# Idle TensorE products ahead of two expert stages, and the modulation sums of the first mixer at other chunks

## The chip, the cores and the metric

The kernel runs on one core of a Trainium2 chip. The metric is the device time of one launch in microseconds. Below, TensorE does the products (PE in the profile, PEld its weight loads), VectorE is DVE, ScalarE is ACT, GpSimd is POOL, and SyncE (SP) issues most of the transfers. Line numbers such as L862 are those of the kernel before.

## The reference, cut to what matters

A backbone of two layers over 512 latent tokens and 256 context tokens, each a row of 1024 numbers. Layer 0 mixes with a Fourier step beside a gated convolution, layer 1 with windowed attention. Each layer ends in a mixture of 32 experts, of which a token uses two. Each layer's shifts, scales and gates come from a modulation vector.

```python
for layer in range(2):
    mod_l = silu(c) @ w_mod[layer] + b_mod[layer]          # six vectors of 1024
    mod_c = silu(c_ctx) @ w_mod[layer] + b_mod[layer]
    hl = modulate(rms_norm(xl, norm_mix_g[layer]), sh1_l, sc1_l)
    # layer 0: p = h @ w_in; y = concat(fourier(a), b * conv(c * hv)) @ w_out
    # layer 1: windowed attention of latent queries, with the context keys in the same softmax
    xl = xl + g1_l * yl
    hl2 = modulate(rms_norm(xl, norm_ffn_g[layer]), sh2_l, sc2_l)
    f = hier_moe(hl2, ...)   # best group of 4, best two of its 8 experts, by two small products
    # each expert: (silu(x @ w1[e]) * (x @ w3[e])) @ w2[e], times the token's gate
    xl = xl + g2_l * f
```

Layer 0 does the same to the context rows. The inputs and outputs are fp32.

## The kernel before, in words

**First mixer.** `proj` multiplies the split weights (a high part `whi` by ScalarE, the rest `wlo` by VectorE, L1253 and L1255) with the split rows. First come four Fourier chunks (`for g in range(4)`, L1309), each with a projection `four_a` and, one chunk later, the transforms `four_b`; then four convolution chunks (`for j in range(4)`, L1330) with three projections each. Between them sit two feeds that work out modulation vectors. `ModFeed.step` (L1037) multiplies a 2 MB block of `w_mod` on TensorE; it has 16 steps. `SumFeed` does the latent half of four vectors of layer 1 on VectorE: each of its 32 steps adds one 512 KB slice of `w_mod`, times a number, into `acc` (L1075), and after eight steps `finish` sums over the partitions with four small products (L1088), adds the bias (L1090) and writes the vector to memory. Both feeds get their blocks through GpSimd's queue, in the order of issue, and a block is requested when the buffer of an earlier one has been read.

**Mixer output and router.** `mixer_out` multiplies with the output weights, tile by tile of 128 tokens, and does for each tile the norm, the router's products (L223) and, in `Route.tiles`, the choice of experts. `Route.tiles` has three parts with a `yield` between them: VectorE makes the masks `M` and their sum `Mb` (to L341); TensorE counts ranks (L347) and VectorE makes one-hot rows from them (L349 to L357); TensorE sums the first slots' tokens into `acc` (`slots`, L281). `tokens` turns that into a table, and `rest`, later, does the other slots, the gates and the expert numbers (L407, L408). `in_order` chains TensorE's and VectorE's instructions there in program order; for what stands outside it, a scheduler with a cost model picks the order.

**Expert stage.** `moe` goes through the experts in pairs (layer 1 has three groups of four as well). Rows are fetched for 128 slots: in layer 0 by an indirect transfer on GpSimd (`gather`, L739), in layer 1 by products with a one-hot matrix (`tokens_slots` L753, `take` L767). `turn` transposes them (L774), then come w1 and w3 (L862), w2 (L933) and the products that add the result to the tokens (L811). Expert weights stream through a ring of eight buffers of 2 MB, two transfers each, all on SyncE's queue (L723) in order; a transfer waits until its buffer has been read, and the first fourteen are also paced, each by the landing of the one two before. For all but the first experts SyncE first loads the expert's number from a table (L706) that `rest` makes. `run` starts a stage.

Of the kernel before, what the change touches and what calls it, by code (L numbers as in the profile page):

```python
# [85 lines left out]
def body(tc, I, out, upto=None, dbg=None):  # L86
# [140 lines left out]
    def carve(*ts):  # L227
# [15 lines left out]

        return f

    class Route:


# [52 lines left out]
        def tiles(self, m0, m1):  # L301

            n, ms = m1 - m0, slice(m0, m1)
            kg, gk, km, d, k, s2 = [x[:, 0:n] for x in (self.kg, self.gk, self.km, self.d, self.k, self.s2)]
            gm, og, mx0, mx1, Mb, Mc = self.gm[:, ms], self.og[:, ms], self.mx[:, 0, ms], self.mx[:, 1, ms], self.Mb, self.Mc
            M, rk = [x[:, :, ms] for x in (self.M, self.rk)]
            R = self.R.rearrange("p c m e -> p (c m e)")[:, 0:n * 64].rearrange("p (c m e) -> p c m e", c=2, m=n)
            lgg = self.lg[:, ms, 0:4]
            le = self.lg[:, ms, 4:36].rearrange("p m (g e) -> p m g e", g=4)

            def w4(a):
                return a[:, :, None].to_broadcast([128, n, 4])

            def w8(a):
                return a[:, :, :, None].to_broadcast([128, n, 4, 8])

            def first():

                V.scalar_tensor_tensor(k.rearrange("p m g e -> p (m g) e"), d.rearrange("p m g e -> p (m g) e"), 0.0,
                                       K("ew")[:, None, :].to_broadcast([128, n * 4, 8]), op0=ALU.is_equal, op1=ALU.mult)  # L320

            V.tensor_reduce(gm, lgg, axis=AX.X, op=ALU.max)
            V.tensor_reduce(mx0, le, axis=AX.X, op=ALU.max)
            V.tensor_tensor(kg, lgg, w4(gm), op=ALU.is_equal)
            V.tensor_sub(d, le, w8(mx0))
            V.tensor_mul(kg, kg, K("gw")[:, None, :].to_broadcast([128, n, 4]))
            first()
            V.tensor_reduce(gk, kg, axis=AX.X, op=ALU.max)
            V.tensor_reduce(km, k, axis=AX.X, op=ALU.max)
            V.tensor_tensor(og, kg, w4(gk), op=ALU.is_equal)  # L330
            for c in range(2):
                V.tensor_tensor(k, k, w8(km), op=ALU.is_equal)
                if c == 0:
                    V.scalar_tensor_tensor(s2, k, -1e30, le, op0=ALU.mult, op1=ALU.add)
                V.tensor_mul(M[:, c].rearrange("p m (g e) -> p m g e", g=4), k, w8(og))
                if c == 0:
                    V.tensor_reduce(mx1, s2, axis=AX.X, op=ALU.max)
                    V.tensor_sub(d, s2, w8(mx1))
                    first()
                    V.tensor_reduce(km, k, axis=AX.X, op=ALU.max)  # L340
            V.tensor_add(Mb[:, ms], M[:, 0], M[:, 1])  # L341
            yield
            pr = self.psum([128, n, 32])
            for m in range(m0, m1):
                w = [(tri, Mb[:, m])] + [(ones, Mb[:, i]) for i in range(m0, m)] + ([(ones, Mc)] if m0 else [])
                for i, (a, b) in enumerate(w):
                    T.matmul(pr[:, m - m0], a, b, start=i == 0, stop=i == len(w) - 1)  # L347
            for c in range(2):
                V.tensor_mul(self.Mv[:, c, 0, ms], M[:, c], K("blk")[:, ms, None].to_broadcast([128, n, 32]))  # L349
            V.tensor_scalar(self.Mv[:, :, 1, ms], M, K("pcol"), None, op0=ALU.mult)  # L350
            V.tensor_mul(R, M, pr[:, None].to_broadcast([128, 2, n, 32]))
            V.tensor_reduce(rk, R, axis=AX.X, op=ALU.add)
            for c in range(2):
                V.tensor_tensor(self.oh[:, c, ms], K("iota")[:, None, 0:64].to_broadcast([128, n, 64]),
                                rk[:, c, :, None].to_broadcast([128, n, 64]), op=ALU.is_equal)
            for m in range(max(m0, 1), m1):
                V.tensor_add(Mc, Mb[:, 0] if m == 1 else Mc, Mb[:, m])  # L357
            yield
            for m in range(m0, m1):
                self.slots(self.acc, m, self.Mv[:, :, :, m], self.early)  # L360
            yield

        def tokens(self):
# [299 lines left out]
    def moe(layer, NT, tb, ring, mp, mps, near):  # L663
# [288 lines left out]
        def run(rest):  # L952
            X[0] = mp.tile([128, 8, 128], F32, name="xt", bufs=2 if both else 1)
            if not near["h2"]:
                near["held"].update({i: gather(0) for i in (13,)})
            one_hot(0)
            if near["h2"]:
                for f in near["lower"]:
                    lo = f()
                    tc.add_manual_dep(lo.ins, near["mark"].ins.name,  # L960
                                      mybir.DependencyInfo(mybir.DependencyClass.NoSync, mybir.DependencyReason.DATA), reason="order")
                    near["mark"] = lo
            oh = tokens_slots(0) if near["h2"] else None
            for hf in range(2):
                xr = take(oh, hf)
            for hf in range(2):
                turn(0, xr, hf)
            if not near["h2"]:
                gather(order[1])
            with tc.issue_after(near["mark"].ins):  # L970
                rest()
            fill()
            for n in range(len(steps)):
                py_ = step(n)
            with in_order(mybir.EngineType.PE, mybir.EngineType.DVE):
                if near["late"]:
                    hi = rows(last, 1, py_, lambda: [add(last, 0, m) for m in range(2)])
                    near["late"](hi, lambda m, hf: add(last, hf, m))
                else:
                    rows(last, 1, py_, lambda: [near["done"](m, 0, add(last, 0, m)) for m in range(2, NT)])  # L980
                    for m in range(NT):
                        near["done"](m, 1, add(last, 1, m))
            if not near["late"]:
                beyond()
# [62 lines left out]
    class SumFeed:  # L1047
# [1 line left out]


        def __init__(self, layer, vectors, room):
            self.layer, self.vectors, self.room = layer, vectors, room
            self.acc = room.tile([128, D], F32, name="acc")
            self.todo = [(v, k) for v in vectors for k in range(8)]
            self.w = []
            self.ld = 0
            for _ in range(2):
                self.load()

        def tile(self):  # L1060
            return self.room.tile([128, D], F32, name="mw", bufs=2)

        def load(self):
            if self.ld < len(self.todo):
# [5 lines left out]
        def step(self):  # L1070
            v, k = self.todo.pop(0)
            self.ld -= 1
            w = self.w.pop(0)
            if k:
                V.scalar_tensor_tensor(self.acc, w, sil[:, k, 0:1], self.acc, op0=ALU.mult, op1=ALU.add)  # L1075
            else:
                V.tensor_scalar(self.acc, w, sil[:, k, 0:1], None, op0=ALU.mult)
            if k == 7:
                self.finish(v)
            self.load()  # L1080

        def finish(self, v):

# [221 lines left out]
    prev = None  # L1305
    load_conv(0)
    pre = proj_pre()
    sums = SumFeed(1, (2, 3, 4, 5), sp)
    for g in range(4):  # L1309
        aT = four_a(g)  # L1310
        if g:
            with tc.issue_after(mm["last"].ins):
                feed.step()
        sums.step()
        if prev is not None:
            four_b(g - 1, prev)
        feed.step()
        sums.step()
        sums.step()
        prev = aT  # L1320
    wo = I["w_out_even"][0].rearrange("(j p) d -> p j d", p=128)

# [7 lines left out]
    for j in range(4):  # L1330
        wr4 = wconv[j]
        pc = proj(lambda k0: wr4[:, k0:k0 + 4, 1, :])
        if prev is not None:
            four_b(3, prev)
            prev = None
            close(fp)
            cp = pool("cp")
            u = cp.tile([128, L + LC + 4], F32, name="ut")
            for c in (0, L + 1, L + 2, L + LC + 3):
                V.memset(u[:, c:c + 1], 0.0)  # L1340
        csb = tp.tile([128, L + LC + 4], F32, name="t3", bufs=2)
        S.copy(csb[:, 0:L + LC], pc)
        feed.step()
        sums.step()
        load_conv(j + 1)
        if j == 3:
            wout = load_wout(0, 1)
# [5 lines left out]
        V.scalar_tensor_tensor(z[:, 1:1 + N2], u[:, 0:N2], cw[:, 0, j:j + 1], z[:, 1:1 + N2], op0=ALU.mult, op1=ALU.add)  # L1353
        V.scalar_tensor_tensor(z[:, 1:1 + N2], u[:, 2:2 + N2], cw[:, 2, j:j + 1], z[:, 1:1 + N2], op0=ALU.mult, op1=ALU.add)
        feed.step()
        sums.step()
        sums.step()
        pb = proj(lambda k0: wr4[:, k0:k0 + 4, 0, :])
        for o, p0, n in segs:
            V.tensor_mul(z[:, o:o + n], z[:, o:o + n], pb[:, p0:p0 + n])  # L1360
        put_y(4 + j, [z[:, o:o + 256] for o in (1, 257, L + 3)])
        feed.step()
        sums.step()
        sums.step()
    close(cp, tp, sp, hp)


    def mixer_out(layer, NT, lhs, raws, whl, x1, psA, psB, hq, rq, mk_route, h2dst, mdp):
# [30 lines left out]
        for hf in range(2):  # L1399
# [67 lines left out]
            with in_order(PE, DVE, chain=chain):  # L1467
# [4 lines left out]
                for g in going:  # L1472
                    for _ in g:
                        pass
        route.md = mds[0]
        route.tokens()
        return route

# [124 lines left out]
    def modulated(m, xn, hf_, psum):  # L1603
# [3 lines left out]
        for hf in range(2):  # L1607
# [7 lines left out]
                else:  # L1615
                    V.tensor_scalar(hf_[:, k, :], p[:, q, :], A1[:, s, k:k + 1], AB[:, s, 0, k:k + 1], op0=ALU.mult, op1=ALU.add)

    near = {"quads": 0, "late": row_scale, "more": kv_weights, "h2": None, "spill": 1, "x1": x1, "xg": mx_[:, 0, :], "grow": [mx_[:, 1, :], mx_[:, 2, :]],
            "iota": slots_iota(mp)}
    G.memset(near["xg"], 0.0)  # L1620
    near["held"] = {13: route.wrote}
# [352 lines left out]
        hs = slice(hf * 512, hf * 512 + 512)  # L1974
        Y.dma_start(out[0, m * 128:(m + 1) * 128, hs], x1[m][:, hs])

    near = {"quads": QUADS, "done": store, "late": None, "held": {}, "h2": h2s, "md": route.md, "lower": route.lower, "spill": 0, "x1": x1, "grow": [mp.tile([128, D], F32, name="grow")], "iota": slots_iota(mp)}
    S.dma_start(near["grow"][0], brow(mod_d[1, 0, 5 * D:6 * D]))
    fill, run = moe(1, 4, tb, ring, mp, mps, near)
    fill(6)  # L1980
# [33 lines left out]
```

## Time and profile before

| what | value |
|---|---|
| median of 3 runs | 1658.29 us (1654.82 to 1658.82) |
| profiled execution | 1657.86 us, of which the span 1655.9 us |
| TensorE busy | 1525.1 us, 92% of the span |
| VectorE busy | 759.7 us, 46% |
| ScalarE busy | 440.3 us, 27% |
| transfers | 503.50 MB, mean 304 GB/s |
| mean granted TensorE clock | 0.965 of 2.4 GHz |

The span runs from the first to the last instruction of the execution that was profiled. Busy shares are averages over stages with different limits: the first mixer runs to about 235 us, its output and router to 350, layer 0's experts to 850, attention to 1100, the second output and router to 1165, layer 1's experts to the end.

### The profile page before, as it was taken

To read this page: it belongs to the slowest core of one execution; us is meant where nothing else is said; L and a number is where in the kernel's file an instruction comes from. 1 tells how busy PE (TensorE), PEld (TensorE's weight loads), DVE (VectorE), ACT (ScalarE), POOL (GpSimd) and SP (SyncE) were. 2 spreads that over 40 slices of the span, in tenths; PEclk is the share of its full clock that TensorE was granted. 3 is DMA by queue.
4 is the path that set the end of the run, shared out by engine and by line. 5 is a ranking of instruction groups with operands and counts; after the bars stand their busy time and mean duration, and the time that the engine had idled before them with its cause. 6 is when DMAs were issued, how large, how long until landed. Compare 5 with 4: busy or idle time off the path is not lost.

```text
span 1655.9 us, 21500 instructions
## 1 busy us (share of the span) xinstructions
PE 1525.1 (92%) x8011; PEld 866.5 (52%) x8011; DVE 759.7 (46%) x1671; ACT 440.3 (27%) x879; POOL 141.7 (9%) x160
## 2 busy tenths in 40 slices
PE   4989997969999999999988989999799999997787
PEld 2757876843444434444447776668444544531332
DVE  4546553784342534333366975555622322320223
ACT  5322221311111111111046577644221222210110
POOL 2522100300000000000033210000000000000000
PEclk9999997979999999999979999999899999998999
DMA  9897672579999999999930121042699999999996
GB/s 387 306 389 246 229 245 82 189 278 424 425 424 424 381 394 424 425 424 424 407 121 1 51 52 52 1 128 76 237 426 427 426 426 427 426 416 427 426 427 260
DMA packets 108832, 503.50 MB, mean 304 GB/s; under 512 B 18784, under 2 KB 33632, under 8 KB 56752
## 3 DMA queue, kind: packets, MB, share of 16 engines
q1 hardware_dynamic: 93600, 447.31, 67.1%
q0 software_dynamic: 11952, 51.55, 8.2%
q10 hardware_dynamic: 3168, 3.17, 0.6%
q8 instruction: 66, 1.08, 0.3%
q14 instruction: 46, 0.38, 0.1%
HBM read 499.30 MB, written 5.32 MB: 305 GB/s over the span
## 4 chain that ended last, share of the span: by engine, by line
PE 34%; DMA 10%; DVE 3%; ACT 2%; issue 1%; SPq 0%; DVEq 0%; ACTq 0%
PE p L862 8%; PE yp L933 5%; DMA w<-in_w_dram 5%; DMA hhi<-in_w_dram 4%; PE A L1715 3%; PE cp L811 3%; PE A L1436 3%; PE tp L767 2%; PE A L1833 2%; PE O L1895 2%; PE B L1880 2%; ACT P L1839 1%; PE tp L774 1%; DVE x L812 1%; DMA w<-in_w_qkv_dram 0%
## 5 line engine op out<-in xcount | busy, mean ns | idle before, releaser
L862 PE MATMUL p<-w,xt 128*64 128x512 f32 (+1 forms) x1024 | 338.5, 611 | 14.3 <-DMA w<-in_w_dram 14.1
L862 PE MATMUL p<-r,xt 128*64 128x512 f32 (+1 forms) x784 | 284.2, 620 | 8.3 <-DMA r<-in_w_dram 7.9
L812 DVE TENSOR_TENSOR x<-x,cp 128x512 f32<-128x512 f32 x224 | 148.1, 685 | 96.5 <-PE cp L811 96.4
L875 DVE TENSOR_TENSOR sg<-sg,p 128x512 f32<-128x512 f32 x29 | 20.0, 688 | 365.9 <-PE p L862 354.9
L811 PE MATMUL cp<-y,ot 128*128 128x512 f32 x616 | 174.5, 419 | 8.3 <-DVE x L812 4.5
L862 PEld LDWEIGHTS p<-w,xt 128*64 128x64 f32 (+1 forms) x1024 | 99.6, 135 | 127.3 <-issue 98.6
L933 PE MATMUL yp<-w,ht 128*64 128x512 f32 (+1 forms) x512 | 158.7, 595 | 2.2 <-DMA w<-in_w_dram 2.2
L862 PEld LDWEIGHTS p<-r,xt 128*64 128x64 f32 (+1 forms) x784 | 84.5, 137 | 144.5 <-issue 124.8
L811 PEld LDWEIGHTS cp<-y,ot 128*128 128x128 f32 x616 | 107.2, 191 | 52.0 <-DVE x L812 26.3
L933 PE MATMUL yp<-r,ht 128*64 128x512 f32 (+1 forms) x368 | 128.7, 595 | 1.3 <-ACT ht L894 0.7
L799 ACT CAST y<-yp 128x512 fp32r<-128x512 f32 x58 | 34.0, 586 | 277.0 <-DVE yp L795 185.5
L1436 PE MATMUL A<-r,r 128*128 128x512 f32 x288 | 71.2, 404 | 2.2 <-ACT r L1402 1.4
L933 PEld LDWEIGHTS yp<-r,ht 128*64 128x64 f32 (+1 forms) x368 | 38.1, 134 | 66.7 <-issue 64.0
L862 PE MATMUL p<-hhi,xt 128*64 128x512 f32 (+1 forms) x128 | 66.0, 672 | 7.1 <-DMA hhi<-in_w_dram 7.1
L933 PEld LDWEIGHTS yp<-w,ht 128*64 128x64 f32 (+1 forms) x512 | 46.4, 131 | 45.6 <-issue 40.1
L1436 PEld LDWEIGHTS A<-r,r 128*128 128x128 f32 x288 | 55.1, 195 | 14.8 <-ACT r L1402 2.3
L1837 DVE CUSTOM_DVE_ANT_0 A<-A,band,nsink 128x640 f32<-128x640 f32 (+1 forms) x56 | 45.4, 831 | 35.4 <-PE A L1833 35.2
L865 ACT ACTIVATE sg<-p 128x512 f32<-128x512 f32 x29 | 17.3, 597 | 157.0 <-PE p L862 157.0
L801 DVE TENSOR_TENSOR y<-yp,y 128x512 fp32r<-128x512 f32 x58 | 40.1, 691 | 40.0 <-ACT y L799 40.0
L797 DVE SCALAR_TENSOR_TENSOR yp<-yp,gs,grow 128x512 f32<-128x512 f32 x26 | 19.7, 759 | 72.4 <-PE yp L933 72.4
L739 POOL DMA_INDIRECT r<-h_d,gi x17 | 17.0, 997 | 411.8 <-PE tp L774 342.4
L862 PE MATMUL p<-hlo,xt 128*64 128x512 f32 (+1 forms) x112 | 51.8, 611 | 0.0
(434 smaller groups left out, 2605.5 us busy)
## 6 DMA issues: line engine op xcount, KB each, us to landing
w<-in_w_dram SPq DMA_DIRECT2D x191, 1024.0 KB, 19.5
r<-in_w_dram SPq DMA_DIRECT2D x143, 1024.0 KB, 19.5
w<-in_w_mod_dram POOLq DMA_DIRECT2D x12, 2048.0 KB, 10.1
hhi<-in_w_dram SPq DMA_DIRECT2D x23, 1024.0 KB, 19.5
hlo<-in_w_dram SPq DMA_DIRECT2D x23, 1024.0 KB, 19.5
mw<-in_w_mod_dram POOLq DMA_DIRECT2D x32, 512.0 KB, 5.2
w<-in_w_in_even_dram SPq DMA_DIRECT2D x13, 512.0 KB, 11.2
w<-in_w_mod_dram SPq DMA_DIRECT2D x3, 2048.0 KB, 12.8
```

Source lines behind the costliest of these rows:

```text
L767: T.matmul(p, oh[:, m, :], near["h2"][m][i][:, hf * 512:hf * 512 + 512], start=n == 0, stop=n == 7)
L799: hi = S.copy(Yr[j, hf][0], ys)
L801: V.tensor_sub(Yr[j, hf][1], ys, Yr[j, hf][0].bitcast(F32))
L811: T.matmul(p, OT[j][:, m * 128:(m + 1) * 128], Yr[j, hf][i], start=n == 0 and i == 0, stop=n == len(js) - 1 and i == 1)
L812: return V.tensor_add(xs, xs, p)
L862: T.matmul(ps[rs], X[b][:, q, rs], W[j, wn, ab][:, q, :], start=q == 0, stop=q == 7)
L933: T.matmul(py_[hf][rs, :], HT[b][:, q % 4, rs], W[j, "w2", ab][:, q % 4, hf * 512:hf * 512 + 512], start=q % 4 == 0, stop=q % 4 == 3)
L1436: T.matmul(ps, lhs(m, a, j), whl[b][:, j, :], start=j == 0 and i == 0, stop=j == 7 and i == 2)
L1715: T.matmul(ps, h[st][:, k, ms], whl[k][b], start=k == 0 and i == 0, stop=k == 7 and i == 2)
L1833: T.matmul(ps[:, o0:o0 + w], qS[G_][:, c, b * 128:(b + 1) * 128], kS[part][:, 2 * G_ + c // 4, k0:k0 + w], start=part == 0, stop=part == 1)
L1837: V.tensor_tensor_reduce(out=ps[:, 0:w], in0=ps[:, 0:w], in1=bnd, op0=ALU.add, op1=ALU.min, scale=1.0, scalar=nsink[:, hd:hd + 1], accum_o ...
L1880: T.transpose(p[:, i, :], Ps[gl * 4 + i][:, t * 128:(t + 1) * 128], ident)
```

## The change

`idle(n, psum)` issues n products of 128 x 256 bf16 columns (the mask `tri` as weight, the identity as moving operand) into a PSUM tile that nothing reads. It is called in the last group of tiles of each router: 30 products ahead of the rank products, 7 ahead of the slot products, and behind these 45 in layer 0 and 5 in layer 1. In layer 1, 4 more stand between the transposes of the first one-hot matrix and the gather products. These and the first transposes of a stage are now chained to TensorE's order of the router.

The 32 sums of `SumFeed` are spread anew. Before, each of the four Fourier chunks had three, each of the four convolution chunks five. Now the feed is opened in the first Fourier chunk, behind that chunk's projection; the four have 0, 1, 2 and 3, the first three convolution chunks 9, 9 and 8, and the last none. From the first convolution chunk on, slices are fetched into four buffers instead of two.

```diff
+    def idle(n, psum):
+        p = psum([128, 256])
+        for _ in range(n):
+            T.matmul(p, tri, ident.bitcast(BF), start=True, stop=True)
...
             V.tensor_add(Mb[:, ms], M[:, 0], M[:, 1])
             yield
+            if m1 == self.NT:
+                idle(30, self.psum)
...
             yield
+            if m1 == self.NT:
+                idle(7, self.psum)
             for m in range(m0, m1):
                 self.slots(self.acc, m, self.Mv[:, :, :, m], self.early)
+            if m1 == self.NT:
+                idle(45 if self.spill else 5, self.psum)
             yield
...
-            oh = tokens_slots(0) if near["h2"] else None
-            for hf in range(2):
-                xr = take(oh, hf)
-            for hf in range(2):
-                turn(0, xr, hf)
+            with in_order(mybir.EngineType.PE, chain=near["chain"]):
+                if near["h2"]:
+                    oh = tokens_slots(0)
+                    idle(4, lambda shape: mps.tile(shape, F32, name="cp", bufs=2))
+                else:
+                    oh = None
+                for hf in range(2):
+                    xr = take(oh, hf)
+                for hf in range(2):
+                    turn(0, xr, hf)
...
     class SumFeed:
-            self.layer, self.vectors, self.room = layer, vectors, room
+            self.layer, self.rooms, self.at = layer, [room], 0
...
+            self.more()
+
+        def more(self, *rooms):
+            self.rooms += rooms
             for _ in range(2):
                 self.load()
 
         def tile(self):
-            return self.room.tile([128, D], F32, name="mw", bufs=2)
+            self.at += 1
+            return self.rooms[self.at % len(self.rooms)].tile([128, D], F32, name="mw", bufs=2)
...
+        def steps(self, n):
+            for _ in range(min(n, len(self.todo))):
+                self.step()
...
-    sums = SumFeed(1, (2, 3, 4, 5), sp)
     for g in range(4):
         aT = four_a(g)
         if g:
             with tc.issue_after(mm["last"].ins):
                 feed.step()
-        sums.step()
+        if g == 0:
+            with tc.issue_after(mm["last"].ins):
+                sums = SumFeed(1, (2, 3, 4, 5), sp)
         if prev is not None:
             four_b(g - 1, prev)
         feed.step()
-        sums.step()
-        sums.step()
+        sums.steps(g)
...
             cp = pool("cp")
+            sums.more(cp)
...
         feed.step()
-        sums.step()
+        sums.steps(3)
...
         feed.step()
-        sums.step()
-        sums.step()
+        sums.steps(3)
...
         feed.step()
-        sums.step()
-        sums.step()
+        sums.steps(3)
```

## Rows read from the trace of the kernel before

**Rows 1.** Stretches of the first mixer, router and layer 0's experts (header: columns).
```profile
core 0: us, PE busy (x) PEld busy (x) DVE busy (x) ACT busy (x) POOL busy (x), PEclk, DMA share, GB/s
...
120.00:233.00 113.00, 113.00 (x676) 93.04 (x675) 67.20 (x99) 24.90 (x44) 18.39 (x33) 1.00 0.68 234
...
338.00:342.00 4.00, 4.00 (x27) 3.63 (x26) 3.48 (x12) 1.32 (x4) 0.00 (x0) 0.50 0.94 376
...
540.00:600.00 60.00, 59.66 (x278) 27.17 (x274) 27.31 (x44) 8.04 (x14) 1.98 (x2) 1.00 0.91 374
```

**Rows 2.** TensorE in order of time, first mixer: start, length, idle before.
```profile
104.44 1.92 PE L1037 MATMUL M<-w,sil 128*32 128x512 f32 x16 [3.40 <-DMA w<-in_w_mod_dram]
107.14 1.05 PE L1088 MATMUL B<-acc,onef 128*32 128x512 f32 x4 [0.77 <-DVE acc L1075]
...
117.17 1.05 PE L1299 MATMUL A<-dl,Z 128*128 128x128 f32 x7 [1.45 <-DVE Z L1287]
...
233.65 1.05 PE L1088 MATMUL B<-acc,onef 128*32 128x512 f32 x4
236.07 1.19 PE L1436 MATMUL A<-r,r 128*128 128x512 f32 x4 [1.37 <-ACT r L1402]
...
257.36 7.01 PE L1389 MATMUL B<-wr,md 128*128 128x36 f32 x32 [9.00 <-DMA md<-mod_d]
```

**Rows 3.** Stretches of the second router and layer 1's experts (columns as rows 1).
```profile
1154.00:1160.00 6.00, 5.48 (x53) 5.03 (x52) 4.19 (x19) 3.14 (x6) 0.00 (x0) 1.00 0.82 298
...
1164.00:1174.00 10.00, 7.75 (x27) 5.70 (x28) 9.70 (x37) 2.29 (x4) 0.00 (x0) 0.50 0.71 274
...
1182.00:1192.00 10.00, 10.00 (x122) 3.90 (x118) 3.01 (x18) 0.60 (x1) 0.00 (x0) 1.00 0.02 7
1192.00:1440.00 248.00, 246.34 (x1163) 117.03 (x1160) 70.62 (x114) 58.04 (x122) 0.00 (x0) 1.00 1.01 425
...
1450.00:1452.00 2.00, 2.00 (x12) 0.57 (x8) 0.69 (x1) 0.56 (x1) 0.00 (x0) 1.00 0.89 324
1452.00:1454.00 2.00, 2.00 (x20) 0.55 (x20) 0.76 (x1) 0.57 (x1) 0.00 (x0) 1.00 0.88 315
```

**Rows 4.** SyncE's queue in layer 1: loads of expert numbers, next weight.
```profile
L706 SPq TENSOR_LOAD <-ex x25: 262/264/284, 1176.3 to 1190.3; - x25
...
1191.01 0.35 SPq L723 DMA_DIRECT2D w<-in_w_dram  x1
```

**Rows 5.** Transfers from 60 to 104 us: count, size, median to landing.
```profile
DMA packets 5754, 16.25 MB, mean 369 GB/s; under 512 B 383, under 2 KB 3455, under 8 KB 4466
...
w<-in_w_mod_dram POOLq DMA_DIRECT2D x6, 2048.0 KB, 9.8
mw<-in_w_mod_dram POOLq DMA_DIRECT2D x9, 512.0 KB, 7.0
```

**Rows 6.** VectorE in order of time ahead of Z at 117 us.
```profile
113.16 1.37 DVE L1090 TENSOR_TENSOR mw<-B,mw 1x512 f32<-1x512 f32 x2
```

**Rows 7.** Chain that ended last, layer 1's start: start, length, what.
```profile
1166.26 1.23 PE tp L753 x4
1168.15 6.54 PE tp L767 x15
...
1194.82 2.15 PE tp L767 x8
```

**Rows 8.** TensorE in order of time, starts of both expert stages.
```profile
346.39 0.21 PE L347 MATMUL B<-w,tri 128*128 128x32 bf16 x1 [3.78 <-DVE w L341]
...
354.76 1.97 PE L774 MATMUL tp<-cst,r 128*128 128x128 f32 x8 [6.34 <-DMA r<-h_d,gi]
356.66 1.12 PE L862 MATMUL p<-w,xt 128*64 128x512 f32 x1
...
357.56 1.04 PE L862 MATMUL p<-w,xt 128*64 128x512 f32 x1
...
1163.50 0.18 PE L347 MATMUL B<-w,tri 128*128 128x32 bf16 x1 [4.01 <-DVE w L341]
...
1177.10 3.65 PE L862 MATMUL p<-w,xt 128*64 128x512 f32 x16
```

More of the change, by code (lines that the diff above doesn't have):

```diff
@@ L1474, in mixer_out @@
                         pass
-        route.md = mds[0]
+        route.md, route.chain = mds[0], chain
         route.tokens()
@@ L1616, in modulated @@
                     V.tensor_scalar(hf_[:, k, :], p[:, q, :], A1[:, s, k:k + 1], AB[:, s, 0, k:k + 1], op0=ALU.mult, op1=ALU.add)
-    near = {"quads": 0, "late": row_scale, "more": kv_weights, "h2": None, "spill": 1, "x1": x1, "xg": mx_[:, 0, :], "grow": [mx_[:, 1, :], mx_[:, 2, :]],
+    near = {"chain": route.chain, "quads": 0, "late": row_scale, "more": kv_weights, "h2": None, "spill": 1, "x1": x1, "xg": mx_[:, 0, :], "grow": [mx_[:, 1, :], mx_[:, 2, :]],
             "iota": slots_iota(mp)}
@@ L1975, in store @@
         Y.dma_start(out[0, m * 128:(m + 1) * 128, hs], x1[m][:, hs])
-    near = {"quads": QUADS, "done": store, "late": None, "held": {}, "h2": h2s, "md": route.md, "lower": route.lower, "spill": 0, "x1": x1, "grow": [mp.tile([128, D], F32, name="grow")], "iota": slots_iota(mp)}
+    near = {"chain": route.chain, "quads": QUADS, "done": store, "late": None, "held": {}, "h2": h2s, "md": route.md, "lower": route.lower, "spill": 0, "x1": x1, "grow": [mp.tile([128, D], F32, name="grow")], "iota": slots_iota(mp)}
     S.dma_start(near["grow"][0], brow(mod_d[1, 0, 5 * D:6 * D]))
```

## The prediction, made before the changed kernel ran

> **What bounds the kernel now.** I read the busy time by stretches first, then TensorE's instructions in order of time around the two places that the change fills, then the chain of waits, and last the transfers with SyncE's own queue, because a faster TensorE is worth something only where no transfer is waited for.
>
> The first mixer is TensorE's. From 120 to 233 us it is busy throughout at full clock [rows 1]; a hole ahead of that stretch, closed, moves all that follows. There are three such holes: 3.40 us for a modulation matrix, 0.77 us for a sum, 1.45 us for the Fourier step's Z [rows 2]. The 9.00 us wait behind the mixer [rows 2] hangs on transfers that start when the mixer's last product has read its operands, so it moves with the mixer and takes nothing back.
>
> Layer 0's expert stage follows TensorE as well: from 540 to 600 us TensorE is busy 59.66 of 60 us while the transfers run at 374 GB/s and not at 425 [rows 1, 3]. What TensorE gains at that stage's start it keeps. Layer 1's stage is different: from 1192 to 1440 us the transfers run at 425 GB/s with a share of 1.01 [rows 3], so it ends by when its stream restarted. The stream stood still from 1182 to 1192 us (share 0.02) [rows 3], and SyncE's queue shows why: 25 loads of expert numbers run on it from 1176.3 to 1190.3 us, and the next weight is issued at 1191.01 [rows 4].
>
> **The change part by part.**
>
> *The sums.* Up to the wait at 104.44 us, nine transfers of 512 KB for sums and six of 2048 KB for TensorE's modulation products had been issued [rows 5]. In the new order two are fetched at the start and one replaces each sum done; by the same point only 1 + 2 sums are done, so five transfers stand where nine stood. The awaited transfer is issued only when its buffer is free, so not all four count. I take two that shared the channels with it: 2 x 0.52 MB, at the 369 GB/s of that stretch [rows 5] 2.8 us, and at 425 GB/s [rows 3] 2.5; 2.6 of the 3.40 go, bounds 0 and 3.40. The 0.77 belongs to the first finished vector, which now ends in the convolution part: gone here. The 1.45 stands behind two additions of that vector's end, 1.37 us together on VectorE [rows 6]: I take 1.37, bounds 0 and 1.45. Saved: 2.6 + 0.77 + 1.37 = 4.74.
>
> Against it: the last vector's products, 1.05 us, stood in a gap, since the next product waited 1.37 us for ScalarE anyway [rows 2]. They move into the stretch without gaps: +1.05. Nine sums now stand in each of three convolution chunks, where five stood. VectorE is busy 67.2 of 113 us there [rows 1], so there is room, and four buffers fetch ahead instead of two; but three sums in a row hold the weight splits that stand behind them on VectorE, and TensorE waits for those. No row shows this. Its bounds are 0 and all that the part saves; I put it at one wait of the size that a sum cost before, +0.77. The part is worth -4.74 + 1.05 + 0.77 = -2.9.
>
> *Price of one idle product.* It has 256 columns. The gather products have 512: at 1168.15 us fifteen take 6.54 us and later eight take 2.15 [rows 7], that is 0.436 us and at most 0.27. Half of that is 0.218 at the low clock and at most 0.134 at the high one (at least 0.109, half of 0.218); I take 0.12. Their weight load I price at nothing, as it runs beside the product before, here as in the gather; uncovered, it is inside the 0.134.
>
> *Layer 0.* TensorE waits 3.78 us for VectorE's mask before the rank products [rows 8]. Thirty idle products fit if the clock is up (3.6 us), but it is not: from 338 to 342 us TensorE is busy 4.00 of 4.00 us at clock 0.50, which is 1.2 GHz [rows 1]. All at that clock they take 6.5 us, 2.8 too many. They stand ahead of the rank products on TensorE, and behind those stand VectorE's token table, the gather and the first transposes. So the delay lies between 0 and 2.8; I take 2.0, nearer to the low clock, because from 1164 to 1174 us it stayed at 0.50 throughout, through gather products from 1168.15 on [rows 3, 7]. Then the 45 products (5.4 us) fit into the gather's 6.34 us [rows 8]. Saved behind it: the eight transposes take 1.97 us, at the high clock about half, of which ScalarE's copies between them leave 0.5; the first expert pairs start 0.90 us apart [rows 8], at the high clock half, so two cold pairs give 0.9; the two small product groups 0.2. 1.6 saved, 2.0 lost: +0.4.
>
> *Layer 1.* Here the clock is still 1.00 when the wait begins [rows 3], so 30 products (3.6 us) fit into its 4.01 us [rows 8], and the clock should hold through the 7, the 5 and the 4. The fifteen gather products then take about 3.3 us less than 6.54. The four transposes at 1166.26, 1.23 us [rows 7], give 0.6, which I leave out, since the number lookup's products stand between and wait for VectorE. So the experts start some 3.3 us before 1177.10 [rows 8]. But SyncE's 25 loads do not hang on the expert products: they come behind a weight that waits for earlier weights to land. So the stream still restarts at 1191. What is left is where the transfers last waited for TensorE: from 1450 to 1454 us they ran at 324 and 315 instead of 425 GB/s [rows 3], which is 0.48 + 0.52 = 1.0 us. That goes: -1.0.
>
> *Sum.* -2.9 + 0.4 - 1.0 = -3.5. The profiled execution took 1657.86 us (span 1655.9), 0.4 below the median of the three runs, 1658.29; 1657.86 - 3.5 = 1654.4.
>
> **The rivals.**
>
> *All holes close.* The mixer loses all 5.6 us of them, pays 1.05, meets no new wait, and layer 0's clock is up before its 30 products (saving 1.6 with no delay): -4.6 - 1.6 - 1.0, 1650.7 us. For it: VectorE's room. Against it: the clock row at 338 us.
>
> *Layer 1's gain arrives whole.* If the schedule lets SyncE's loads come earlier with the expert number, the restart moves with TensorE: -2.9 + 0.4 - 3.3, 1652.1 us. Against it: the weight ahead of them is paced by landings.
>
> *The sums only move their waits.* If three sums in a row cost TensorE 0.36 us at each of eight places, the mixer's 2.9 are gone: 1657.3.
>
> *Transposes let the clock go.* TensorE at 338 to 342 us did transposes and router products, always busy, and the clock stood at 0.50 [rows 1]; but from 1154 to 1160 us it did the like and kept 1.00 [rows 3]. If they don't hold it, the clock falls again between the 5 and the 4 in layer 1 and ahead of the experts in layer 0: 1.0 and 1.4 us of the gains are lost, 1656.8. This is a rule of the Trainium skill ("TensorE: Matmul & The Clock Gate", Part 4, on PE-mode transposes): transposes don't count as TensorE work in the way products do. By that rule the time would be those 1656.8; the two rows disagree on it, so I give it little.
>
> *Slower: the idle products run at the low clock.* If they do not raise or hold it, layer 0's 30 cost 2.8 us, its 45 take 9.8 instead of 6.34 (3.5 more), and layer 1's 30 take 6.5 instead of 4.01 (2.5), with SyncE's number loads late by as much. +8.8 - 2.9: 1663.8. It decides from where the clock still stands at 0.50 when the 45 begin. Against it: the expert products, as dense, do raise it.
>
> **How the numbers follow.** Chances: the forecast 0.46 (its own range 1651.5 to 1657.5), all holes close 0.20, layer 1 whole 0.14, the sums' waits 0.08, transposes 0.06, low clock 0.06. A measurement of this kernel tells about 0.3% (5 us) from no change, so below 1653.3 counts as faster, above 1663.3 as slower. Faster: nearly all of the second (0.18), most of the third (0.10), a fifth of the first (0.10): 0.38. Slower: the last and a little for worse waits: 0.07. Same: 0.55. The range leaves out the low clock and the far ends of the others: 1648.5 to 1660.5.
>
> **What would show it.** In the new profile the wait at 104 us is below 1 us and those at 107 and 117 are gone, with the convolution stretch still without gaps. Layer 0's rank products start some 2 us behind their mask and its expert products 0.43 us apart from the first pair. In layer 1 the clock reads 1.00 from 1160 us on, the experts start about 3 us sooner after the router, and the first weight behind the 25 loads comes as late after it as before. The prediction is wrong if TensorE gets holes in the convolutions, if the stream in layer 1 restarts earlier relative to the router's end, or if the clock is down in the 45.

## The result and the profile after

The changed kernel takes 1636.52 us (1634.59 to 1639.26, 4 runs) against 1658.55 us for the kernel before on the same chip: a ratio of 0.9877, 95% interval 0.9855 to 0.9898. The two medians are 22.0 us apart, and the ratio stands for 20.4 us. The forecast was 1654.4, so the gain is some six times the 3.5 us that it summed. The profiled execution took 1636.33 us with a span of 1634.5; TensorE's mean granted clock is 0.978 instead of 0.965.

Stretches of the changed kernel, with the busy time of each engine, the granted clock and the transfers:

```profile
core 0: us, PE busy (x) PEld busy (x) DVE busy (x) ACT busy (x) POOL busy (x), PEclk, DMA share, GB/s
100.00:120.00 20.00, 20.00 (x128) 15.05 (x127) 11.74 (x27) 6.28 (x12) 3.77 (x6) 1.00 0.74 282
120.00:229.00 109.00, 109.00 (x649) 86.35 (x648) 67.18 (x92) 23.15 (x40) 21.93 (x39) 1.00 0.74 269
240.00:260.00 20.00, 15.79 (x65) 12.71 (x65) 7.52 (x13) 0.00 (x0) 0.00 (x0) 0.83 0.74 207
260.00:280.00 20.00, 20.00 (x98) 16.83 (x97) 9.22 (x15) 4.97 (x8) 0.00 (x0) 1.00 0.17 63
328.00:334.00 6.00, 6.00 (x31) 4.42 (x31) 4.51 (x24) 1.28 (x1) 0.00 (x0) 0.53 0.89 362
1143.00:1149.00 6.00, 4.52 (x38) 3.13 (x39) 5.70 (x20) 1.65 (x2) 0.00 (x0) 1.00 0.97 384
1170.00:1420.00 250.00, 248.34 (x1173) 119.18 (x1172) 71.80 (x116) 59.21 (x124) 0.00 (x0) 1.00 1.01 425
```

From 100 to 120 us TensorE has no hole left; the three of [rows 2] are gone, and none has come into the stretch to 229 us. From 260 to 280 us it runs at full clock, where the kernel before had 0.76:

```profile
240.00:260.00 20.00, 11.00 (x50) 9.24 (x49) 4.83 (x10) 0.00 (x0) 0.00 (x0) 0.82 0.86 263
260.00:280.00 20.00, 20.00 (x79) 17.04 (x79) 6.26 (x11) 0.00 (x0) 0.00 (x0) 0.76 0.13 53
```

Layer 1's expert stage still goes at 425 GB/s, as in [rows 3].

TensorE of the changed kernel in order of time (start, length, idle before), behind the mixer and at the start of both expert stages:

```profile
232.19 11.18 PE L1462 MATMUL A<-r,r 128*128 128x512 f32 x48 [2.35 <-ACT r L1428]
246.11 1.97 PE L1415 MATMUL B<-wr,md 128*128 128x36 f32 x16 [2.74 <-DMA md<-mod_d]
...
328.34 6.05 PE L250 MATMUL B<-cst,tri 128*128 128x256 bf16 x30
334.23 0.18 PE L355 MATMUL B<-w,tri 128*128 128x32 bf16 x1
...
335.94 5.09 PE L250 MATMUL B<-cst,tri 128*128 128x256 bf16 x45
342.40 1.16 PE L786 MATMUL tp<-cst,r 128*128 128x128 f32 x8 [1.38 <-DMA r<-h_d,gi]
...
343.78 0.64 PE L874 MATMUL p<-w,xt 128*64 128x512 f32 x1 [0.21 <-ACT xt L791]
...
344.26 0.59 PE L874 MATMUL p<-w,xt 128*64 128x512 f32 x1
...
1139.49 3.44 PE L250 MATMUL B<-cst,tri 128*128 128x256 bf16 x30
1143.65 0.19 PE L355 MATMUL B<-w,tri 128*128 128x32 bf16 x1 [0.72 <-DVE w L347]
...
1153.89 1.08 PE L874 MATMUL p<-w,xt 128*64 128x512 f32 x4
```

The wait for md behind the mixer was 9.00 us [rows 2] and is 2.74. What the idle products do shows here too: in layer 0 the 30 run at the low clock (6.05 us, granted 0.53 in that stretch), the 45 at the high one, and the first expert pairs stand 0.43 to 0.48 us apart instead of 0.90 [rows 8].

Marks on the path divide the two profiles into stages: SyncE's first load of x (it waits for the mixer's last product), the first w1 product of layer 0, the start of its last w2 product, SyncE's load of the second router's group bias, the first w1 product of layer 1, the end of the span. All in us:

| stage | before | after | difference |
|---|---|---|---|
| to the first load of x | 233.81 | 229.93 | -3.9 |
| mixer output, router, to layer 0's experts | 122.85 | 113.85 | -9.0 |
| layer 0's experts | 485.01 | 484.08 | -0.9 |
| attention, to the second router's loads | 257.99 | 251.97 | -6.0 |
| to layer 1's experts | 77.44 | 74.06 | -3.4 |
| the rest | 478.80 | 480.61 | +1.8 |

The sum is -21.4. Some 15 us of it stand in two stages to which the forecast gave 0.4 us or nothing. SyncE's queue shows what changed in the first of them. The kernel before (start, length of the issue, what is loaded):

```profile
233.81 1.77 SPq L1490 DMA_DIRECT2D x<-in_x_dram  x4
...
236.64 0.38 SPq L1395 DMA_DIRECT2D a<-mod_d  x1
237.12 0.46 SPq L1395 DMA_DIRECT2D h<-mod_d  x1
237.63 1.24 SPq L1395 DMA_DIRECT2D b<-mod_d  x1
242.28 0.33 SPq L723 DMA_DIRECT2D w<-in_w_dram  x1
...
244.07 8.57 SPq L1374 DMA_DIRECT2D br<-in_b_router_g_dram  x1
...
254.40 0.38 SPq L1383 DMA_DIRECT2D md<-mod_d  x1
```

And the changed kernel:

```profile
229.93 1.77 SPq L1516 DMA_DIRECT2D x<-in_x_dram  x4
...
233.33 3.74 SPq L1399 DMA_DIRECT2D wr<-in_w_router_e_dram  x1
237.11 3.26 SPq L1400 DMA_DIRECT2D br<-in_b_router_g_dram  x1
...
242.03 0.38 SPq L1409 DMA_DIRECT2D md<-mod_d  x1
...
243.45 0.46 SPq L1421 DMA_DIRECT2D a<-mod_d  x1
...
246.00 0.71 SPq L1421 DMA_DIRECT2D b<-mod_d  x1
```

Before, three rows of 512 KB (a, h and b) and a 1 MB weight stood ahead of the router's matrices and of md, an 8 KB vector; md was issued 20.6 us behind the first x. Now they stand behind it, and md is issued 12.1 us behind x. Not all of the difference is bytes. In the kernel before, SyncE also stood still for 3.3 us at the weight, whose buffer VectorE was reading for its split of the output weights until 242.26 us, and every load behind the weight stood with it (the first line is SyncE's wait: in total, times, longest):

```profile
SPq L723 <- DVE r L1403: 3.3, 1, 3.3
237.35 4.91 DVE L1403 TENSOR_TENSOR r<-w,r 128x512 fp32r<-128x512 f32 x8
```

No line of the diff touches these loads. They stand outside the hand-written order, so the scheduler with its cost model places them, and moving the sums made it place them otherwise (e1 below). The same holds for the work in attention. There the traces have two orders: TensorE, VectorE and ScalarE each go through their instructions in one sequence in the kernel before and in e7, and in another in the changed kernel and the eleven other runs, where in e4 and e5 a single instruction of ScalarE's and of VectorE's stands elsewhere.

### The profile page after: what moved, and what is told of

It is laid out like the page before. It is cut to its first block, busy times and chain, and to the rows that moved or that the text cites. A ratio compares the mean times of both kernels' runs of the same rounds, so it can differ in the third digit from the quotient of the medians.

```text
span 1634.5 us, 21757 instructions
## 1 busy us (share of the span) xinstructions
PE 1532.6 (94%) x8139; PEld 871.5 (53%) x8139; DVE 755.8 (46%) x1671; ACT 440.1 (27%) x879; POOL 141.5 (9%) x160
## 4 chain that ended last, share of the span: by engine, by line
PE 33%; DMA 10%; DVE 3%; ACT 3%; issue 1%; SPq 0%; ACTq 0%; DVEq 0%
PE p L874 9%; PE yp L945 5%; DMA w<-in_w_dram 5%; DMA hhi<-in_w_dram 5%; PE cp L823 3%; PE A L1462 3%; PE A L1741 3%; PE tp L779 2%; PE O L1921 2%; PE A L1859 2%; PE B L1906 2%; ACT P L1865 1%; PE tp L786 1%; DMA w<-in_w_qkv_dram 1%; DVE x L824 1%
## 5 line engine op out<-in xcount | busy, mean ns | idle before, releaser
L874 PE MATMUL p<-r,xt 128*64 128x512 f32 (+1 forms) x784 | 280.9, 611 | 10.1 <-DMA r<-in_w_dram 9.7
L809 DVE SCALAR_TENSOR_TENSOR yp<-yp,gs,grow 128x512 f32<-128x512 f32 x26 | 19.7, 758 | 74.2 <-PE yp L945 74.2
## 6 DMA issues: line engine op xcount, KB each, us to landing
w<-in_w_mod_dram POOLq DMA_DIRECT2D x12, 2048.0 KB, 10.4
```

The costliest lines, as they stand in the source:

```text
L874: T.matmul(ps[rs], X[b][:, q, rs], W[j, wn, ab][:, q, :], start=q == 0, stop=q == 7)
```

## The experiments

**Each half alone.** `e1_sums_only` takes the diff's `SumFeed` part (the new places, the late opening, `more`), `e2_idle_only` the rest:

```diff
# e1: kernel before, and of the diff only
+            sums.more(cp)
+        sums.steps(3)
...
# e2: kernel before, and of the diff only
+                idle(30, self.psum)
+                idle(7, self.psum)
+                idle(45 if self.spill else 5, self.psum)
...
```

> The kernel before with the new places of the sums alone: no idle product, no chain. Theory A (order of queues): the places of the sums change the order in which the planner puts SyncE's loads behind the mixer (the router's small matrices and the modulation vector md ahead of the three 512 KB rows and the weight) and the order of ScalarE's and VectorE's work in the attention stage; mixer -3.9, behind the mixer about -10.5, attention about -6: 1638 us, with TensorE's wait for md near 2.7 us instead of 9.00. Theory B (the forecast's, that only the closed holes count): 1658.5 - 2.9 = 1655.6 us. Theory C (the idle products bring most of it): within 4 us of before.

Measured: 1638.56 us, ratio 0.9894 (0.988 to 0.9909). The mixer ends at 228.90, md is issued at 240.68, and attention takes 252.24 us.

> The kernel before with the idle products and the chain alone; the sums stay. The planner leaves SyncE's loads behind the mixer as before, but has the attention stage in the new order. Theory A: wait for md stays at 9.0 us; attention about -6; layer 0's start between -1 and +2; layer 1's start -2 to -3: 1649 us (1647 to 1653). Theory B (forecast's idle terms, +0.4 and -1.0, and nothing in attention): 1657.9 us. Theory C (idle products bring most of the 22 us): below 1645.

Measured: 1650.01 us, ratio 0.9963 (0.995 to 0.9977). TensorE waits 7.69 us for md, with a, h and b ahead of it as before; attention takes 248.35 (this profiled execution, 1644.61 us, was the fastest of six). So the sums' new places bring nearly all the gain, and not through the mixer alone; the idle products' run gained mostly in attention, where no idle product stands. The two gains don't add up to the whole, since each half by itself already gives attention its new order.

**The queue alone, from both sides.** `e3_md_first` orders a, h, b and the third weight behind md in the kernel before; `e4_md_last` puts a, h and b ahead of the router's loads in the changed one.

```diff
# e3, in row() and in fill()
+            if layer == 0 and eng is Y and name in ("a2", "h2", "b2"):
+                tc.add_manual_dep(i.ins, mdl[0, 1].ins.name, ...)
+                    if len(issued) == 3 and near["h2"] is None:
+                        tc.add_manual_dep(issued[-1], mdl[0, 1].ins.name, ...)
# e4, in mixer_out, ahead of wr
...
+            with in_order(mybir.EngineType.SP, chain=spc):
+                for n_, bufs, s_, c in (("a2", 1, 0, 4), ("h2", 3, 1, 4), ("b2", 1, 0, 3)):
+                    early[n_] = hq.tile([128, D], F32, name=n_, bufs=bufs)
+                    Y.dma_start(early[n_], brow(mod_d[0, s_, c * D:(c + 1) * D]))
...
```

> The kernel before, with the three 512 KB rows a, h, b and the third expert weight ordered behind the second modulation vector md on SyncE's queue, as they stand in the changed kernel; nothing else is edited (the attention stage falls into the new order here too). Theory A: the mixer ends as before, the wait for md falls from 9.00 to about 3, the clock stays up through 250 to 270 us: about -10 by the stage of the second router loads, -6 more in attention: 1642 us. Theory B (the wait for md moves with the mixer and is not set by the queue): the wait stays near 9 and the time within 3 us of before, or -6 if attention's order counts.

Measured: 1644.22 us, ratio 0.9929 (0.9916 to 0.9942). TensorE in e3, the product that waits for md:

```profile
249.39 1.97 PE L1392 MATMUL B<-wr,md 128*128 128x36 f32 x16 [1.30 <-DMA md<-mod_d]
```

The mixer ends as before (233.53), md is issued 11.7 us behind x, the wait is 1.30 us, and the stage to layer 0's experts takes 112.47 us instead of 122.85. That stage in the kernel before, and in e3 (columns as in the stretches above):

```profile
233.81:356.66 122.85, 99.23 (x515) 83.46 (x511) 79.73 (x242) 27.76 (x56) 19.30 (x15) 0.85 0.55 182
```

```profile
233.53:346.00 112.47, 95.01 (x515) 79.43 (x511) 79.94 (x242) 27.64 (x56) 19.39 (x15) 0.91 0.64 208
```

Both have 515 products. Of the 10.4 us, 6.2 are idle time (122.85 - 99.23 = 23.6 against 112.47 - 95.01 = 17.5), and 4.2 are the same products at a higher mean clock, 0.91 instead of 0.85. Behind the wait the clock stood at 0.76 from 260 to 280 us in the kernel before, with TensorE busy throughout, and stands at 1.00 in e3, so the long wait was paid a second time in products at the low clock:

```profile
240.00:260.00 20.00, 17.05 (x76) 13.85 (x75) 8.15 (x15) 0.00 (x0) 0.00 (x0) 0.91 0.88 249
260.00:280.00 20.00, 20.00 (x98) 16.85 (x97) 9.85 (x16) 4.97 (x8) 0.00 (x0) 1.00 0.35 119
```

> The changed kernel with the three rows a, h, b put ahead of the router's matrices and md on SyncE's queue, as in the kernel before (the weight stays behind md); all else as in the changed kernel. Theory A: 1.5 MB at about 400 GB/s come ahead of md, so its wait grows by about 4 us from 2.7, and a part of the cold clock behind it comes back: +4 to +8 us, 1640.5 to 1644.5. Theory B: no change, 1636.5.

Measured: 1642.98 us, ratio 0.9921 (0.9909 to 0.9934), above the changed kernel by 6.5 us in the medians and 7.3 in the ratios. In e4:

```profile
249.97 6.37 PE L1422 MATMUL B<-wr,md 128*128 128x36 f32 x29 [6.20 <-DMA md<-mod_d]
```

md is issued 17.7 us behind x instead of 12.1, 5.6 us for 1.5 MB, and the wait is 6.20. The queue's order sets the wait, and it does so ahead of md's issue: from that issue to the product that waits for md pass 3.0 us in the kernel before, 4.1 in e3 and in the changed kernel and 3.6 in e4. No run in the kernel before moves the rows without the weight, so of the 8.5 us (20.6 - 12.1) only the 3.3 us that SyncE stood at the weight can be told from the time that the bytes cost. The Trainium skill ("DMA: Bandwidth & Descriptors", Two DMAs through the same engine are not ordered) says that within one queue of one DMA engine descriptors start in order. These runs don't show that rule at work, since the delay stands before md is issued at all.

**Attention's order alone.** `e5_seven` adds the chain and 7 idle products in layer 0 to the kernel before.

```diff
# e5: of the idle products only
+                idle(7 if self.spill else 0, self.psum)
```

> The kernel before with the chain and the 7 idle products ahead of layer 0's slot products, nothing else: no other idle product, the sums in their old places. Seven products of some 0.2 us can take at most 1.5 us. But the planner then puts ScalarE's, VectorE's and TensorE's work in the attention stage in the order that the changed kernel has; SyncE's loads behind the mixer stay as before. Theory A (the order in attention is worth about 6 us by itself): 1650.5 us (1648 to 1653), the stage from the last expert product to the second router loads some 252 us instead of 258. Theory B (attention's 6 us came from something else in the changed kernel, say the clock or what layer 0 left behind): within 2 us of before, 1655 to 1658.

Measured: 1651.22 us, ratio 0.9975 (0.9964 to 0.9985), 4.1 us less. The queue behind the mixer is as before (wait for md 8.7 us); attention takes 249.77 us instead of 257.99. The chain alone does not do it, since e7 has the chain too and keeps the old order. Attention in the kernel before (columns as in the stretches above):

```profile
841.67:1099.66 257.99, 238.25 (x1402) 175.09 (x1400) 178.00 (x446) 165.14 (x360) 37.78 (x27) 0.95 0.15 44
```

In e5, and in e2:

```profile
843.21:1092.98 249.77, 232.58 (x1402) 170.35 (x1400) 173.02 (x446) 165.19 (x360) 37.31 (x27) 0.99 0.15 46
```

```profile
840.75:1089.10 248.35, 230.19 (x1402) 168.53 (x1400) 172.75 (x446) 165.31 (x360) 37.28 (x27) 1.00 0.15 46
```

In the changed kernel:

```profile
827.86:1079.83 251.97, 235.15 (x1402) 171.96 (x1400) 173.01 (x446) 165.31 (x360) 37.31 (x27) 0.97 0.15 46
```

TensorE has 1402 instructions everywhere. Idle time falls from 19.7 to 17.2 us in e5 and to 18.2 in e2; the rest is the clock (0.95, 0.99, 1.00). In the changed kernel attention has 235.15 us busy at 0.97 and 16.8 idle: 2.9 us of its 6.0 are waits and 3.1 clock. With the old order the profiles show 257.99 and 255.46 (e7), with the new one 248.35 to 252.24 in twelve. The new order is worth some 4 us by e5's time and 5.6 by the means of these profiles, and the clock's part in it differs from kernel to kernel; theory A's 6 us were more than e5's time shows.

**What the idle products do by layer.** `e6_no_layer0_idle` is the changed kernel with layer 0's left out, `e7_layer1_idle` the kernel before with only layer 1's.

```diff
# e6, and e7 on the kernel before
-                idle(30, self.psum)
+                idle(0 if self.spill else 30, self.psum)
...
```

> The changed kernel without the 30, 7 and 45 idle products of layer 0; layer 1's 30, 7, 5 and 4 stay, the sums too. Theory A (as in the first runs: in layer 0 the 30 run at the low clock and put the rank products off by about 2.3 us, and only 1.0 comes back in the first expert pairs): 1635 us, 1.3 below the changed kernel's 1636.5. Theory B (the idle products pay in layer 0): 1638 to 1640.

Measured: 1636.25 us, ratio 0.9881 (0.9866 to 0.9897): the changed kernel's time. From the first x to layer 0's last w2 product it takes 597.9 us, as the changed kernel does (112.58 + 485.34 against 113.85 + 484.08): what the first pairs gain, the 30 lose.

> The kernel before with the chain and layer 1's idle products alone (30, 7, 5 and 4). The order behind the mixer and in attention stays as before. Theory A: layer 1's experts start 3.3 us earlier behind the router, and 1.6 to 2.8 us of it reach the end, because the weight stream restarts some 2 us earlier: 1654 us. Theory B (the forecast: the stream does not move): -1.0, 1655.5. Theory C (layer 1's gain arrives whole): -3.4, 1653.

Measured: 1654.09 us, ratio 0.9994 (0.9983 to 1.0005), -1.0 us with an interval from -2.8 to +0.8. From the second router's loads to the end, the nine profiles with layer 1's idle products show 553.4 to 556.3 us, 554.6 in the mean, and the five without them 555.4 to 556.3, 555.9 in the mean: 1.3 us, with ranges that overlap.

**The mixer without the queue's change.** `e8_two_buffers` has the sums in their new places, but no `more(cp)`; the scheduler then leaves a, h and b ahead of md.

```diff
# e8: e1 without
-            sums.more(cp)
```

> The kernel before with the sums in their new places but with two slice buffers throughout (the two more of the convolution chunks are left out). By the order of the built program SyncE's loads behind the mixer then stand as in the kernel before (a, h, b ahead of md), while attention has the new order. Theory A: TensorE gains in the mixer what it gains in the changed kernel (-4, if two buffers suffice), waits about 9 us for md as before, and attention gives 6: 1647 us. Theory B (the loads' order followed from where the sums stand, and md's wait is short by that alone): 1638.

Measured: 1647.07 us, ratio 0.9939 (0.9926 to 0.9952). The mixer ends at 229.18, as early as with four buffers, and TensorE is busy 20.00 of 20 us from 100 to 120 us. Then:

```profile
252.56 3.81 PE L1397 MATMUL B<-wr,md 128*128 128x36 f32 x17 [8.35 <-DMA md<-mod_d]
```

So the closed holes and the short wait for md are two things. The sums' places close the holes with two buffers as well; what the two more buffers change in the profiles is the order of the loads. In e8 md is issued 20.4 us behind x, as in the kernel before: with the old order the wait did move with the mixer.

**Versions that go on from there.** `e9_after_again` is the changed kernel; `e10_only_45` has 28 idle products in layer 0's gather wait in place of its 30, 7 and 45; `e11_md_before_x` is e10 with md and the router's matrices ahead of the six rows x; `e12_md_before_x_all_idle` is that with the changed kernel's own idle products.

```diff
# e10 and e11: the changed kernel with
-                idle(30, self.psum)
+                idle(0 if self.spill else 30, self.psum)
-                idle(7, self.psum)
+                idle(0 if self.spill else 7, self.psum)
-                idle(45 if self.spill else 5, self.psum)
+                idle(28 if self.spill else 5, self.psum)
# e11 and e12: x is loaded behind md
...
+    def x_loads():
+        for m in range(6):
+            i = Y.dma_start(x1[m], xsrc[m])
+            tc.add_manual_dep(i.ins, mdl[0].name, ...)
...
+            if layer == 0 and s == 0:
+                mdl.append(i.ins)
+                x_loads()
```

> The changed kernel itself once more, on the chip of the next two, so that they can be held against it: 0.988 of before, 1635 to 1637 us.

Measured: 1637.06 us, ratio 0.9878 (0.9859 to 0.9896).

> The changed kernel with layer 0's 30 and 7 idle products left out and 28 instead of the 45 behind the slot products, inside the gather's wait of 6.3 us; all else as it is. Theory A (the 30 only put the rank products off; what raises the clock for the first expert pairs can stand in the gather's wait): layer 0's experts start as early as without idle products and their first pairs stand 0.43 us apart: 1.0 to 1.5 us below the changed kernel. Theory B (28 at the low clock overrun the wait): experts as late as in the changed kernel, no gain. Theory C (the gather's wait is not long enough for the clock to come up): as without idle products, no gain.

Measured: 1637.7 us, ratio 0.9884 (0.9862 to 0.9906), no gain. TensorE of e10:

```profile
333.15 0.21 PE L357 MATMUL B<-w,tri 128*128 128x32 bf16 x1 [3.78 <-DVE w L349]
...
334.97 6.07 PE L252 MATMUL B<-cst,tri 128*128 128x256 bf16 x28
...
341.31 1.16 PE L788 MATMUL tp<-cst,r 128*128 128x128 f32 x8 [0.27 <-DMA r<-h_d,gi]
...
342.70 0.64 PE L876 MATMUL p<-w,xt 128*64 128x512 f32 x1 [0.21 <-ACT xt L793]
...
811.61 1.82 PE L825 MATMUL cp<-y,ot 128*128 128x512 f32 x4 [3.32 <-PEq L576]
```

The 28 fit into the wait, and layer 0's experts start 1.3 us earlier behind the first x than in the changed kernel's first profile (112.54 against 113.85) and 0.95 earlier than in e9, as early as with none of layer 0's idle products (112.58 in e6). But the branch at the end of that stage (L576, `with tc.If`) holds TensorE 3.32 us, where it holds the changed kernel 1.53, and the gain is given back there. The same place in the changed kernel:

```profile
810.86 1.17 PE L823 MATMUL cp<-y,ot 128*128 128x512 f32 x4 [1.53 <-DVEq L574]
```

Theory A's early start is shown, its time is not.

> As the run before (28 in the gather's wait alone), and the router's matrices and the first md now stand ahead of the six 512 KB rows x on SyncE's queue instead of behind them. Theory A (md's wait is set by the bytes ahead of it on the queue): the 2.7 us that TensorE still waits for md are gone, and the clock does not drop behind it: 2 to 4 us below the run before, 1631 to 1633.5 us. Theory B (md waits for its own write to memory or for buffers, not for the queue): no gain; or x comes late for VectorE's first addition and the output tiles wait, a loss of 1 to 3 us.

Measured: 1633.58 us, ratio 0.9849 (0.9832 to 0.9866). TensorE no longer waits for md and is busy 20.00 of 20 us at clock 1.00 from 240 to 260 and from 260 to 280 us. The branch still costs 3.4 us.

> The changed kernel with all its idle products (30, 7 and 45 in layer 0), and the router's matrices and the first md ahead of the six rows x on SyncE's queue. Theory A (the md wait and the low clock behind it are what the queue still cost, and layer 0's idle products are worth nothing either way): as the run before, 1632 to 1634 us, with no wait for md. Theory B (the 30 are worth something once the clock is up at their start): 1630 us. Theory C (they cost their 1.3 us at the rank products and more, since experts start earlier than weights come): 1635 us.

Measured: 1631.0 us, ratio 0.9839 (0.9822 to 0.9856), the fastest of all and faster than the changed kernel by some 6 us. The branch costs 1.5 us here. Its difference to e11 is within the intervals.

## Why the prediction was wrong

**The step that failed** is "The 9.00 us wait behind the mixer [rows 2] hangs on transfers that start when the mixer's last product has read its operands, so it moves with the mixer and takes nothing back". It took the order of SyncE's loads as given. With that order it was right: in e8 the mixer ends 4.6 us sooner and the wait is still 8.35. But the wait was set by four loads of 2.5 MB ahead of md, and the scheduler made another order: 10.4 us in e3 with nothing else changed in that stage, 9.0 in the changed kernel, where layer 0's idle products stand in the same stage. No rival named it either; the one that spoke of a schedule looked only at layer 1.

**The missing term.** Attention got no term, since the diff touches nothing in it. It became 6.0 us shorter, again by another order of instructions that were not edited; e5 has this without the queue's change, for 4.1 us.

**The sums: mechanism right, size too small.** The forecast had -2.9; the first x comes 3.9 us earlier in the changed kernel's profile, and in the mean 5.0 us earlier over seven profiles with the new places (229.4) against five with the old (234.4). All three holes closed (3.40 + 0.77 + 1.45), the last vector's products cost their 1.05 us, which makes -4.6; the allowance of 0.77 for new waits was not needed, and the 3.40 went whole instead of 2.6. The rival "all holes close" had this part right. "The sums only move their waits" is refuted by the stretch from 120 to 229 us.

**Layer 0: right, with both sizes too large.** Forecast +0.4, as 2.0 lost less 1.6 saved. The 30 ran at the low clock as feared (6.05 us, not 6.5), the rank products came 1.3 us later behind the mixer than in e10 (I took 2.0), the 45 fitted, the pairs started at the high clock; e6 puts the net at nothing, with 1.3 us lost ahead of the experts and 1.3 won back in their stage.

**Layer 1: size right, one reason not.** Forecast -1.0; the profiles show -1.3 and e7 -1.0, and neither is far clear of nothing. The experts start 3.4 us sooner after the router (3.3 was worked out), and most of it does not reach the end. But the stream's restart did move, which the prediction named as a sign of being wrong: the first weight behind the number loads is issued 36.9 us behind the first of four loads r of expert weights in the kernel before (the weight at 1191.01 [rows 4]) and 34.6 in the changed kernel:

```profile
1154.09 9.06 SPq L723 DMA_DIRECT2D r<-in_w_dram  x4
```

```profile
1134.27 7.90 SPq L735 DMA_DIRECT2D r<-in_w_dram  x4
...
1168.90 0.35 SPq L735 DMA_DIRECT2D w<-in_w_dram  x1
```

In the mean it is 34.7 us over the nine profiles with layer 1's idle products and 35.6 over the five without (34.3 to 36.9). So some 1 us of the 2.3 goes with the idle products, and the rest is no more than these profiles differ among themselves.

**The clock's rivals** did not come. In layer 1 the granted clock reads 1.00 through the transposes between the 5 and the 4 idle products, so "transposes let the clock go" has no price here. The rule that it rests on is in the Trainium skill ("TensorE: Matmul & The Clock Gate", Part 4): transposes don't count as work of TensorE in the same way. Idle products stand close on both sides, so these rows don't test that rule. The low clock in layer 0's 30 was over before the 45 began.

**What stays open.** Why the scheduler's cost model turns these two orders is not settled. That small edits do it is shown: two more buffers turn the loads (e8 against e1), seven short products turn attention (e5). The clock's share in attention, 0.97 to 1.00 with nearly one and the same order, is read off and not explained. The mixer's 5.0, the queue's 9.0, attention's 5.6 and layer 1's 1.3 us add up to 20.9 against 20.4 measured, but no run has the closed holes by themselves; the nearest are e8 and e5, 10.1 and 4.1 us below the kernel before, so 6.0 apart.

## What to carry to other kernels

Where a scheduler places what the program leaves free, a change has a second effect: the order of everything that it did not touch. Compare the order of each engine's queue in both built programs before summing the edit's own terms, DMA queues first. A small load that TensorE waits for belongs ahead of large ones on its queue, by an explicit order, and ahead of any load that must wait for its buffer: here 8 KB behind 2.5 MB cost 10.4 us, of which 4.2 were the low clock after the wait. So a wait can be paid twice, once idle and once in the products behind it. Filling a wait with idle products brought nothing where they ran at the low clock ahead of work on the path (layer 0), and about 1 us where they ran at the high one (layer 1).

## What the hardware showed unexpectedly

The time that TensorE loses at the conditional branch at the end of layer 0 is 1.5 us in twelve of these programs' profiles and 3.3 to 3.4 in the two with 28 idle products (e10, e11), and the profile names TensorE's own sequencer as what ended the longer wait. The program is the same at that place, and e6 without layer 0's idle products has the short wait too. The Trainium skill ("Runtime: NRT & Kernel Launch", Instruction fetch mechanics) says that a taken branch out of the fetched window stalls for a fetch. No run here shows that the longer wait is such a stall.

SyncE stood 8.57 us in the issue of a load of 2 KB (br, in the kernel before) and 3.26 us in the changed kernel, and everything behind it on the queue with it. And attention's 1402 TensorE instructions were busy between 230.2 and 238.3 us, at mean clocks of 1.00 and 0.95; the runs with one and the same sequence there still read from 0.97 to 1.00, and what decides it is not shown.
